# A closer scheduler model and a higher rank for readings of banks, in a hybrid MLA + DeltaNet block on one Trainium2 core

## The chip, the cores and the metric

The kernel runs on one core of a Trainium2 chip. A core has five engines with instruction streams of their own: TensorE (PE: matmuls, with the weight loads PEld beside them), VectorE (DVE), ScalarE (ACT), GpSimd (POOL) and SyncE (SP), which issues transfers. The metric is the device time of one execution in microseconds (us).

## The reference

One layer of a decoder block with 512 tokens, width 2048 and float32 throughout:

```python
def block(x, c, p):                         # x (512, 2048)
    sh_a, sc_a, gt_a, sh_f, sc_f, gt_f = split(silu(c) @ w_mod + b_mod)
    h = rmsnorm(x) * (1 + sc_a) + sh_a
    cq, ckv, kpe, q, k, v, z, b, a, ga, gb = split(h @ w_in)
    ya = mla(cq, ckv, kpe) @ ...            # 8 heads, causal softmax, low-rank q and kv, rotary part
    yb = gdn(conv_silu(q, k, v), z, b, a)   # gated DeltaNet, 8 heads, chunks of 64
    x  = x + gt_a * ((sigmoid(ga) * ya + sigmoid(gb) * yb) @ w_o)
    h2 = rmsnorm(x) * (1 + sc_f) + sh_f
    g, u = split(h2 @ w_gate_up)            # 2 x 5632
    return x + gt_f * ((silu(g) * u) @ w_down)
```

## The kernel before, in words

TensorE multiplies float32 values as pairs: each operand is split into a rounded part `hi` and a rest `lo`, and a product is three matmuls (hi x hi, hi x lo, lo x hi). A weight tile is loaded from memory into a buffer `raw` (5 of them); ScalarE makes `hi` by a cast (`halves`, L263) and VectorE makes `lo = raw - hi` (L264); there are 4 buffers each for `hi` and `lo`. The 16 row blocks of the width are called k. The gate and up projections (`big(s)`, s = 1 to 10), w_o and w_down use Strassen's seven products on halves, which need sums of weight tiles (L1826, L2014) ahead of the split (L1847/1848, L2022/2023).

The work is written as Units (load, split, matmuls, then `post`) which a `Driver` emits in turn: weights are loaded and split a few units ahead, and side chains (statistics, the DeltaNet's solve, attention, normalization) are stepped on after every 12 matmuls. Matmul results lie in 8 PSUM banks, which VectorE or ScalarE has to read ("evict") before the bank is used again. Side results that TensorE itself reads stand on the same two engines.

The order on each engine is set in two ways. TensorE, GpSimd and SyncE are pinned: their instructions keep the order of the program text. VectorE and ScalarE are not: when the kernel is built, the Tile scheduler lists their instructions by priority on a model of the machine, and then the order is fixed. An engine runs its instructions strictly in that order, and waits at the first one whose inputs aren't there.

The steps that the change and the prediction touch:
- start: the parts of w_mod are multiplied by a broadcast `cbc` (L435) and summed (`mod_sum`, L449); `scaled_h` makes h from x and scale (`hh` on ScalarE, L506, `hl` on VectorE, L508); the first weight is split in two parts (L307).
- normalized tokens: when the row norm `r_all` is there, `full_h` (L513, 515, 516) makes the full h for all 16 k.
- low-rank norm: squares of cq and ckv (L991), the copies out of the banks (L992), a scale `rs` by Newton steps (L417, `rsqrt` L229 to 233), its use (L1001); then TensorE transposes ckv (`cT`).
- DeltaNet: the solve of small triangles (`fsX`, `fsT`, L820/822), `T` assembled by copies (L868/869) from its results, which return by DMA; sums `acc` of the convolution (L396, 398).
- attention: softmax (L1187 to 1193), transposes (L1204), values.
- w_o: `add_gated` (L1432) adds the bank to x, squares (L1442/1444) follow, and TensorE sums them (`hss`), from which `part_rstd` makes the row norm of the second half; h2 is normalized (`h2_gen`).
- big(s): the evictions `after` (L1865 to 1879); in `strassen`, `after` (L2038).
- end: `token_unit` squares x (L2377) and scales xo (L2350).

Of the kernel before, what the change touches and what calls it, by code (L numbers as in the profile page):

```python
# [11 lines left out]
AF = mybir.ActivationFunctionType  # L12
ALU = mybir.AluOpType
# [16 lines left out]
AHEAD = 2  # L30
LOADS = 4
GROUP = 12


class Unit:
# [136 lines left out]
def block_kernel(ctx: ExitStack, tc: tile.TileContext, a: dict, out, out_t):  # L172
    nc = Core(tc, PINNED)
# [16 lines left out]
    def S(s, dt=F32):  # L190
        return slots.tile([P, 512], dt, tag="s", name=nm(s))
# [15 lines left out]
    def tok(j):  # L207
        return slice(j * P, (j + 1) * P)

    def h4(ap):  # L210
        return ap.rearrange("p (h d) -> p h d", h=4)

# [67 lines left out]
    def fm_set(name, loads, width, kt, x, done, ks=None, lo_eng=None, st=None, small=False, cols=slice(0, T), alone=False, late=False,  # L280
               in_parts=()):
        widths = [min(P, width - o) for o in range(0, width, P)]
        st = {} if st is None else st

        def unit(k0, nk):
            box = {}

            def start():
                box["raw"] = fetch(loads(k0, nk), width, nk, small)

            def split():
                box["w"] = halves(box.pop("raw"), width, nk, nc.gpsimd if lo_eng and k0 % 4 == 0 else None, small)

            if in_parts and k0 == 0:
                def start():
                    raw = box["raw"] = raws.tile([P, nk, width], F32, tag="raw", name=nm("raw"))
                    for dst, src in loads(k0, nk):
                        for cs in in_parts:
                            load(dst(raw)[:, :, cs], src[:, :, cs])

                def split(between):
                    raw = box.pop("raw")
                    hi = his.tile([P, nk, width], F32R, tag="hi", name=nm("hi"))
                    lo = los.tile([P, nk, width], F32R, tag="lo", name=nm("lo"))
                    box["w"] = hi, lo
                    for i, cs in enumerate(in_parts):
                        nc.scalar.copy(hi[:, :, cs], raw[:, :, cs])  # L307
                        if i == 0:
                            between[0]()
                        nc.vector.tensor_tensor(lo[:, :, cs], raw[:, :, cs], hi[:, :, cs].bitcast(F32), ALU.subtract)  # L310
                        if i == 0:
                            between[1]()

            def pre():
                if k0 == 0 and cols.start == 0:
                    st["ps"] = [PS(name) for _ in widths]

            mms = []
            for kk in range(nk):
                k = k0 + kk  # L320
                for j, wd in enumerate(widths):
                    sl = slice(j * P, j * P + wd)
                    mms += three(
                        lambda j=j, wd=wd: st["ps"][j][:wd, cols],
                        lambda kk=kk, sl=sl: box["w"][0][:, kk, sl], lambda kk=kk, sl=sl: box["w"][1][:, kk, sl],
                        lambda k=k: x(k)[0], lambda k=k: x(k)[1],
                        k == 0, k == kt - 1)

            def post():
                if k0 + nk == kt and done is not None:  # L330
                    done(st["ps"])
                    drv.hold()

            return Unit(start, split, mms, pre, post, alone=alone, late=late and k0 + nk == kt)

        return [unit(k0, nk) for k0, nk in ks or [(k, 2) for k in range(0, kt, 2)]]

    def tm_set(name, loads, kt, x, done, nk=2, ts=tuple(range(NT)), lo_eng=None, weight=1, alone=False, xt=None):
        st = {}
        if xt is None:  # L340
            def xt(k, t):
                return [v[:, tok(t)] for v in x(k)]

        def unit(k0):
            box = {}

            def start():
                box["raw"] = fetch(loads(k0, nk), 512, nk)

            def split():  # L350
                box["w"] = halves(box.pop("raw"), 512, nk, nc.gpsimd if lo_eng and k0 % 4 == 0 else None)

            def pre():
                if k0 == 0:
                    st["ps"] = {t: PS(name) for t in ts}

            mms = []
            for kk in range(nk):
                k = k0 + kk
                for t in ts:  # L360
                    mms += three(
                        lambda t=t: st["ps"][t][:],
                        lambda k=k, t=t: xt(k, t)[0], lambda k=k, t=t: xt(k, t)[1],
                        lambda kk=kk: box["w"][0][:, kk, :], lambda kk=kk: box["w"][1][:, kk, :],
                        k == 0, k == kt - 1)

            def post():
                if k0 + nk == kt:
                    done(st["ps"])
                    drv.hold()  # L370

            return Unit(start, split, mms, pre, post, weight=weight, alone=alone)

        return [unit(k0) for k0 in range(0, kt, nk)]
# [787 lines left out]
    def attention():  # L1162
# [5 lines left out]
        def scores(i):  # L1168
# [8 lines left out]
            if qb == 3:  # L1177
                del QN[h], KN[h], qpT[h]
                if h == 7:
                    kpT.clear()  # L1180

        def softmax(i):
            h, qb = items[i]
            N = (qb + 1) * P
            ps = box[i].pop("ps")
            m, s, r = (sm[:, i, j:j + 1] for j in range(3))
            nc.vector.tensor_tensor(ps[:, tok(qb)], ps[:, tok(qb)], neg, ALU.add)  # L1187
            nc.vector.tensor_reduce(m, ps[:, 0:N], AX.X, ALU.max)
            nc.vector.tensor_scalar(m, m, -scale, None, op0=ALU.mult)
            p = S("P")  # L1190
            nc.scalar.activation(p[:, 0:N], ps[:, 0:N], AF.Exp, bias=m, scale=scale, accum_out=s)
            nc.vector.reciprocal(r, s)
            nc.vector.tensor_scalar(p[:, 0:N], p[:, 0:N], r, None, op0=ALU.mult)
            box[i]["p"] = p

        def transposes(i):
            h, qb = items[i]
            N = (qb + 1) * P
            p = box[i].pop("p")
            ps = PS("pT")  # L1200
            for kb in range(qb + 1):
                nc.tensor.transpose(ps[:, tok(kb)], p[:, tok(kb)], ident)
            s = S("pT")
            (nc.scalar.copy if i % 2 else nc.vector.tensor_copy)(s[:, 0:N], ps[:, 0:N])  # L1204
            box[i]["pT"] = s

        def values(i):
            h, qb = items[i]
            s = box[i].pop("pT")
            if qb == 0:  # L1210
                yps[h] = PS("yT")
            for kb in range(qb + 1):
                mm(yps[h][:, tok(qb)], V[h // 4][kb][:, tok(h % 4)], s[:, tok(kb)], start=kb == 0, stop=kb == qb)
            if qb == 3:
                yT[h] = hilo(yps.pop(h)[:], "y")
                if h % 4 == 3:
                    del V[h // 4]
# [189 lines left out]
    x2 = [[None] * 8 for _ in range(2)]  # L1407
    s_ffn, sh_ffn, gt_mix, gt_ffn, gt_neg, gt_mneg = (C(n, [P, 16]) for n in ("s_ffn", "sh_ffn", "gt_mix", "gt_ffn", "gt_neg", "gt_mneg"))
# [29 lines left out]
    def squares(q, seg, eng):  # L1438
# [6 lines left out]
        else:  # L1445
            st.append(s)

    def part_rstd(segs):

        ps = PS("hss")  # L1450
# [37 lines left out]
    def half_sets(name, loads, x, done):  # L1488
# [3 lines left out]
        def unit(h, k0):  # L1492
# [20 lines left out]

            def post():
                if k0 + 2 == KT:
                    done(h, st[h])
                    st[h] = None
                    drv.hold()

# [208 lines left out]
    def half_of(tile_, k):  # L1728
        return tile_[:, 256 * (k % 2):256 * (k % 2) + 256]
# [10 lines left out]
    def start_h2(h):  # L1740
        return lambda: h2c.append(drv.add(h2_gen(h)))

    def h2_gen(h):

        yield 3 if h else 1
        diag = part_rstd([HALF[h]])
        yield 6 if h else 4
        r = spread(*diag)
        for q in range(8):
            f = S("h2f")  # L1750
            for k in (2 * q, 2 * q + 1):
                nc.vector.scalar_tensor_tensor(half_of(f, k), half_of(x2[h][q], k), s_ffn[:, k:k + 1], r, op0=ALU.mult, op1=ALU.mult)
                nc.scalar.activation(half_of(f, k), half_of(f, k), AF.Identity, bias=sh_ffn[:, k:k + 1])
            x2[h][q] = None
            h2f[h][q] = f
            h2T[h][q] = hilo(f[:], "h2")
            h2n[h] = 2 * q + 2
            yield 2

    w_gu, w_dn = a["w_gate_up"][0], a["w_down"][0]  # L1760
# [38 lines left out]
    def big(s):  # L1799
# [64 lines left out]
        def tt(o, x, y):  # L1864
            nc.vector.tensor_tensor(o, x, y[:], ALU.add)  # L1865

        def after(c, t):
            if c == "m1":
                nc.scalar.copy(v[t], ps["m1"][t][:])
# [126 lines left out]
    def strassen(w, c1, c0, products, ready, outputs, freed):  # L1996
# [6 lines left out]
        def unit(k):  # L2003
# [28 lines left out]

            res = {}

            def after(c):
                def tt(name, x, y, op):
                    s_ = res[name] = euvw[0][:, "euvw".index(name), :] if name in "euvw" else S(name)[:]
# [491 lines left out]
```

## Time and profile before

| quantity | before |
|---|---|
| runs, us | 2731.93, 2739.36, 2734.11 (median 2734.11) |
| span of the profiled execution, us | 2731.7 |
| TensorE busy, us | 2705.7 (99%) |
| VectorE busy, us | 2098.3 (77%) |
| ScalarE busy, us | 1204.9 (44%) |
| GpSimd busy, us | 258.8 (9%) |
| memory read and written, MB | 476.62 and 83.89 |

The page gives the span of one profiled execution, which is 2.4 us under the median of the runs. Busy is the time in which an engine had an instruction under way; matmuls overlap at their ends, so that a busy TensorE is not one at its peak rate. Start times in the rows count from the start of the span. In a row, "out<-in" are the names of the tiles, and the bracket at its end is the idle time of the engine before it and what ended that.

### The profile page before, as it was taken

Reading aid. Unit: us, or ns where it says so; the run is one execution under the profiler, and the core shown is the slowest. Engines: PE = TensorE matmul, PEld = TensorE weight load, DVE = VectorE, ACT = ScalarE, POOL = GpSimd, SP = SyncE. Lnnn points to the kernel's source line nnn. Section 1 sums busy time; section 2 is a strip of 40 time slices with the busy share of each in tenths; the row PEclk is TensorE's granted clock in tenths of the full one; section 3 lists DMA queues with packets and bytes.
Section 4 is the critical chain, followed back from the end, with each engine's and each line's share of the span. In section 5 each row is a group of like instructions: output and inputs, shape, how many; then the busy total and the mean of one; then the engine's idle time right before and its main releaser. Section 6 shows DMA issues by size and latency. Waiting matters only on the chain.

```text
span 2731.7 us, 41089 instructions
## 1 busy us (share of the span) xinstructions
PE 2705.7 (99%) x15304; PEld 2351.8 (86%) x15304; DVE 2098.3 (77%) x3361; ACT 1204.9 (44%) x1717; POOL 258.8 (9%) x361
## 2 busy tenths in 40 slices
PE   9999999999999999999999999999999999999998
PEld 7888788888888888889999888888888888998997
DVE  8784656677977886788787877778787777877877
ACT  3443432442344343234473444444444446446445
POOL 0000011102101000001000000000000103113113
PEclk9999999999999999999999999999999999999999
DMA  9896455646666978725854556665655668569565
GB/s 364 302 357 215 143 177 173 190 144 185 198 187 194 315 253 313 258 78 131 268 185 136 195 201 208 204 208 198 212 190 198 214 212 208 132 194 202 126 190 178
DMA packets 315489, 562.20 MB, mean 206 GB/s; under 512 B 40772, under 2 KB 120916, under 8 KB 315288
## 3 DMA queue, kind: packets, MB, share of 16 engines
q1 hardware_dynamic: 264776, 458.99, 51.6%
q0 software_dynamic: 31872, 74.76, 10.6%
q10 hardware_dynamic: 18640, 25.83, 2.7%
q8 instruction: 120, 1.97, 0.3%
q14 instruction: 81, 0.66, 0.1%
HBM read 476.62 MB, written 83.89 MB: 205 GB/s over the span
## 4 chain that ended last, share of the span: by engine, by line
PE 90%; DVE 4%; DMA 3%; issue 2%; ACT 1%; SPq 0%; DVEq 0%; ACTq 0%; POOL 0%
PE m L155 41%; PE gb L155 6%; PE v L155 4%; PE gu L155 3%; PE z L155 3%; PE ya L155 3%; PE k L155 3%; PE q L155 3%; PE yb L155 3%; PE dn L155 3%; PE s L155 3%; PE ckv L155 2%; PE cq L155 2%; PE wo L155 1%; PE qk L155 1%
## 5 line engine op out<-in xcount | busy, mean ns | idle before, releaser
L263 ACT CAST hi<-raw 128x1024 fp32r<-128x1024 f32 x249 | 258.8, 1041 | 538.9 <-DMA raw<-in_w_in_dram 164.9
L264 DVE TENSOR_TENSOR lo<-raw,hi 128x1024 fp32r<-128x1024 f32 x249 | 302.6, 1216 | 202.4 <-ACT hi L263 197.6
L1847 ACT CAST hi<-raws 128x512 fp32r<-128x512 f32 (+1 forms) x240 | 218.6, 911 | 328.0 <-PE m L155 269.2
L1848 DVE TENSOR_TENSOR lo<-raws,hi 128x512 fp32r<-128x512 f32 (+1 forms) x240 | 247.4, 1042 | 83.9 <-ACT hi L1847 83.6
L155 PE MATMUL m<-xh,lo 128*128 128x256 f32 x1088 | 308.4, 283 | 1.3 <-DVE lo L2023 1.3
L155 PE MATMUL m<-xh,hi 128*128 128x256 f32 x1088 | 308.1, 283 | 1.5 <-ACT hi L2022 1.5
L155 PE MATMUL m<-xl,hi 128*128 128x256 f32 x1088 | 307.9, 283 | 0.0
L449 DVE CUSTOM_DVE_ANT_0 rawm<-rawm,cbc 128x1024 f32<-128x1024 f32 x192 | 232.1, 1230 | 2.0 <-DMA rawm<-in_w_mod_dram 1.7
L155 PEld LDWEIGHTS m<-xh,lo 128*128 128x128 f32 x1088 | 208.8, 192 | 2.0 <-DVE lo L2023 1.9
L155 PEld LDWEIGHTS m<-xh,hi 128*128 128x128 f32 x1088 | 208.9, 192 | 1.7 <-ACT hi L2022 1.7
L155 PEld LDWEIGHTS m<-xl,hi 128*128 128x128 f32 x1088 | 208.9, 192 | 0.1
L155 PE MATMUL m<-hi,h2h 128*128 128x512 f32 x480 | 190.1, 396 | 0.0
L155 PE MATMUL m<-hi,h2l 128*128 128x512 f32 x480 | 187.2, 390 | 0.0
L155 PE MATMUL m<-lo,h2h 128*128 128x512 f32 x480 | 187.2, 390 | 0.0
L2022 ACT CAST hi<-sums 128x1024 fp32r<-128x1024 f32 x88 | 92.2, 1048 | 134.4 <-PE m L155 102.4
L2023 DVE TENSOR_TENSOR lo<-sums,hi 128x1024 fp32r<-128x1024 f32 x88 | 107.4, 1220 | 45.5 <-ACT hi L2022 45.4
L1847 ACT CAST hi<-sums 128x1024 fp32r<-128x1024 f32 x80 | 84.2, 1053 | 109.4 <-PE m L155 104.5
L1848 DVE TENSOR_TENSOR lo<-sums,hi 128x1024 fp32r<-128x1024 f32 x80 | 97.6, 1220 | 26.7 <-ACT hi L1847 26.1
L155 PEld LDWEIGHTS m<-hi,h2l 128*128 128x128 f32 x480 | 90.1, 188 | 19.0
L155 PEld LDWEIGHTS m<-hi,h2h 128*128 128x128 f32 x480 | 90.2, 188 | 18.5 <-DVE euvw L1865 0.7
L155 PEld LDWEIGHTS m<-lo,h2h 128*128 128x128 f32 x480 | 90.3, 188 | 17.5
L2022 ACT CAST hi<-raws 128x768 fp32r<-128x768 f32 x88 | 73.4, 835 | 66.8 <-PE m L155 48.1
(581 smaller groups left out, 7418.3 us busy)
## 6 DMA issues: line engine op xcount, KB each, us to landing
raws<-in_w_gate_up_dram SPq DMA_DIRECT2D x400, 256.0 KB, 3.6
rawm<-in_w_mod_dram SPq DMA_DIRECT2D x192, 512.0 KB, 5.4
raw<-in_w_in_dram SPq DMA_DIRECT2D x143, 512.0 KB, 4.6
raws<-in_w_down_dram SPq DMA_DIRECT2D x128, 256.0 KB, 3.9
s_dram<-raws POOLq DMA_DIRECT2D x80, 256.0 KB, 2.3
raws<-s_dram SPq DMA_DIRECT2D x80, 256.0 KB, 3.3
rawa<-in_w_in_dram SPq DMA_DIRECT2D x32, 512.0 KB, 4.6
raws<-in_w_o_dram SPq DMA_DIRECT2D x48, 256.0 KB, 3.1
```

Source lines behind the costliest of these rows:

```text
L155: return self.tc.keep_in_program_order(f(*args, **kwargs))
L263: nc.scalar.copy(hi[:], raw[:])
L264: (lo_eng or nc.vector).tensor_tensor(lo[:], raw[:], hi[:].bitcast(F32), ALU.subtract)
L449: r = nc.vector.tensor_tensor_reduce(raw, raw, c, 1.0, 0.0, ALU.mult, ALU.add, parts[:, k, half:half + 1])
L1847: nc.scalar.copy(hi[:], src)
L1848: nc.vector.tensor_tensor(lo[:], src, hi[:].bitcast(F32), ALU.subtract)
L2022: nc.scalar.copy(hi[:], src)
L2023: nc.vector.tensor_tensor(lo[:], src, hi[:].bitcast(F32), ALU.subtract)
```

## The change

The list of edits: (1) the scheduler is told to use a closer model of the machine's time (`schedule_with_timeline_sim=True`); (2) a wrapper `soon` lifts the priority of what it wraps by 600 (`SOON`): the readings of banks (`done` of the sets, `after` in big and strassen), softmax, transposes and values of attention, the row norm's `part_rstd`, and the normalization of the tokens h2, whose body becomes a function `normalize`. The pinned engines keep their order, and no operation is added or removed: between the two built programs 736 VectorE and 196 ScalarE instructions stand at another place.

```diff
+SOON = 600
...
+    def soon(f):
+
+        def g(*args, **kwargs):
+            with tc.high_priority(SOON):
+                return f(*args, **kwargs)
+        return g
...
             def post():                      # fm_set; tm_set alike
                 if k0 + nk == kt and done is not None:
-                    done(st["ps"])
+                    soon(done)(st["ps"])
                     drv.hold()
...
+        @soon
         def softmax(i):
...
+        @soon
         def transposes(i):
...
+        @soon
         def values(i):
...
+    @soon
     def part_rstd(segs):
...
             def post():                      # half_sets
                 if k0 + 2 == KT:
-                    done(h, st[h])
+                    soon(done)(h, st[h])
...
+    @soon
+    def normalize(h, q, r):
+        f = S("h2f")
+        for k in (2 * q, 2 * q + 1):
+            nc.vector.scalar_tensor_tensor(half_of(f, k), half_of(x2[h][q], k), s_ffn[:, k:k + 1], r, op0=ALU.mult, op1=ALU.mult)
+            nc.scalar.activation(half_of(f, k), half_of(f, k), AF.Identity, bias=sh_ffn[:, k:k + 1])
+        x2[h][q] = None
+        h2f[h][q] = f
+        h2T[h][q] = hilo(f[:], "h2")
+        h2n[h] = 2 * q + 2
...
         for q in range(8):
-            f = S("h2f")
...
+            normalize(h, q, r)
             yield 2
...
+        @soon
         def after(c, t):                     # big
...
+            @soon
             def after(c):                    # strassen
...
-    with tile.TileContext(nc) as tc:
+    with tile.TileContext(nc, schedule_with_timeline_sim=True) as tc:
```

More of the change, by code (lines that the diff above doesn't have):

```diff
@@ L368, in post @@
                 if k0 + nk == kt:
-                    done(st["ps"])
+                    soon(done)(st["ps"])
                     drv.hold()
@@ L1749, in h2_gen @@
         for q in range(8):
-            f = S("h2f")
[L1751 to L1757, printed above, removed]
+            normalize(h, q, r)
             yield 2
```

## The prediction

> **What bounds the kernel now.** I read the header and the busy totals of the page first, then the chain of work that ended last, then the waits of TensorE, then a table of windows over the places where the order moves.
>
> ```profile
> span 2731.7 us, 41089 instructions
> PE 2705.7 (99%) x15304; PEld 2351.8 (86%) x15304; DVE 2098.3 (77%) x3361; ACT 1204.9 (44%) x1717; POOL 258.8 (9%) x361
> PE 90%; DVE 4%; DMA 3%; issue 2%; ACT 1%; SPq 0%; DVEq 0%; ACTq 0%; POOL 0%
> ```
>
> TensorE (PE) is busy for 2705.7 of 2731.7 us, so at most 26 us could ever be won by reordering the other engines, and some of that is the start and the end, where no matmul can run. VectorE (DVE) is at 77%, not a bound on average. The waits of TensorE for other engines, as (total, times, longest), show how little is left:
>
> ```profile
> PE hss L155 <- DVE sq L1444: 2.2, 1, 2.2
> PE dn L155 <- DVE g L2038: 1.7, 1, 1.7
> ...
> PE cq L155 <- ACT sz L962: 0.9, 1, 0.9
> ```
>
> These are single waits. An order that served TensorE perfectly would win a few such waits. An order that serves it badly in one place can lose more there than all of them together, because a matmul that comes late is never made up by an engine that is 99% full. The windows show where VectorE has no room (columns: window, length, then busy and count of PE, PEld, DVE, ACT, POOL, then granted clock, DMA share, GB/s):
>
> ```profile
> 160.00:206.00 46.00, 45.04 (x199) 36.93 (x198) 44.13 (x65) 22.18 (x29) 2.13 (x4) 1.00 0.99 367
> 690.00:750.00 60.00, 60.00 (x325) 49.56 (x323) 57.76 (x154) 20.20 (x37) 6.79 (x10) 1.00 0.69 210
> ...
> 1358.00:1362.00 4.00, 4.00 (x21) 4.00 (x22) 2.52 (x5) 0.09 (x1) 0.00 (x0) 0.58 0.68 221
> 1400.00:2255.00 855.00, 854.97 (x4128) 720.03 (x4127) 669.59 (x786) 391.90 (x482) 65.97 (x121) 1.00 0.60 198
> ```
>
> At 160 to 206 and at 690 to 750 VectorE is busy for 96% of the time. There, whatever is put in front of a step delays that step by its full length. In the big loop (1400 to 2255) it has 22% free.
>
> **The change, part by part.** No operation is added or removed. Laid side by side, the two built programs have the same instructions on each engine; TensorE, SyncE and GpSimd keep their order to the instruction, 736 VectorE and 196 ScalarE instructions stand elsewhere. So every cost is a delay: the length of what now stands in front of a step, less the slack that step had. I went through the places where the new order puts other work ahead of something that TensorE reads.
>
> *The start.* ScalarE now has the split of the first weight (hi L307, which waits for its DMA) ahead of the third and fourth part of cbc, and VectorE has the two sums L449 of the next k ahead of the first hl.
>
> ```profile
> 8.46 0.41 ACT L307 CAST hi<-raw 128x256 fp32r<-128x256 f32 x1 [1.25 <-DMA raw<-in_w_in_dram]
> ...
> 7.55 1.23 DVE L449 CUSTOM_DVE_ANT_0 rawm<-rawm,cbc 128x1024 f32<-128x1024 f32 x1
> 11.19 0.74 DVE L508 SCALAR_TENSOR_TENSOR hl<-xT,s_mix,hh 128x512 fp32r<-128x512 f32 x1
> ...
> 11.99 0.50 PE L155 MATMUL s<-hl,hi 128*128 128x512 f32 x1 [0.53 <-DVE hl L508]
> ```
>
> The second half of the first L449 waits for cbc until about 10.75 instead of 7.55 (3.2 later), two L449 at 1.15 come in between: hl ends some 4.9 later, TensorE goes on at 16.9 instead of 11.99. This is not a term of its own, because the next place is paced by VectorE and the DMAs and swallows it.
>
> *Normalized tokens at 160 to 190 us.* When r_all arrives, full_h runs for 16 k: L513 scales x (16 times) and L516 makes hl. Before, only four of each were done when the third lo of the next weights (L264) was made.
>
> ```profile
> 162.49 2.07 DVE L513 SCALAR_TENSOR_TENSOR xT<-xT,s_mix,r_all 128x512 f32<-128x512 f32 x3
> 164.48 1.22 DVE L264 TENSOR_TENSOR lo<-raw,hi 128x1024 fp32r<-128x1024 f32 x1
> 165.62 0.74 DVE L516 SCALAR_TENSOR_TENSOR hl<-xT,sh_mix,hh 128x512 fp32r<-128x512 f32 x1
> ...
> 177.26 1.23 DVE L264 TENSOR_TENSOR lo<-raw,hi 128x1024 fp32r<-128x1024 f32 x1 [1.87 <-ACT hi L263]
> ...
> 178.71 0.39 PE L155 MATMUL ga<-hh,lo 128*128 128x512 f32 x1
> ...
> 185.28 0.51 PE L155 MATMUL ga<-hh,lo 128*128 128x512 f32 x1 [0.96 <-DVE lo L264]
> ```
>
> Now all 16 L513 and 12 L516 stand ahead of that lo: 12 + 8 = 20 more. Three L513 take 164.48 - 162.49 = 1.99, so 0.663 each: 13.3 us. VectorE idled 1.87 before the lo at 177.26, which is filled: 11.4 later. TensorE read that lo 0.2 after its end: 11.2 late. The idle 0.96 at 185.28 closes, since the later tiles are then ready: +10.2, the start's 4.9 within it.
>
> *ckv and the solve, 734 to 765 us.* ScalarE now has the cast hi L263, which waits for a buffer that TensorE frees, ahead of the four L991 (squares of ckv); the scale rs of L417 follows, and L1001 applies it.
>
> ```profile
> 735.15 0.59 ACT L991 ACTIVATE junk<-ckv 128x512 f32<-128x512 f32 x1
> 740.83 1.06 ACT L263 CAST hi<-raw 128x1024 fp32r<-128x1024 f32 x1 [2.33 <-PE z L155]
> ...
> 735.86 2.60 DVE L992 COPY ckv<-ckv 128x512 f32<-128x512 f32 x4 [1.06 <-ACT junk L991]
> 738.38 0.16 DVE L417 TENSOR_SCALAR rs<-st_c 128x4 f32<-128x4 f32 x1
> 740.12 0.74 DVE L398 SCALAR_TENSOR_TENSOR acc<-rawa,sh_mix,acc 128x512 f32<-128x512 f32 x1
> 740.86 1.08 DVE L868 COPY T<-T 32x256 f32<-32x256 f32 x1
> 746.98 1.64 DVE L1001 TENSOR_SCALAR ckv<-ckv,rs 128x512 f32<-128x512 f32 x4
> ...
> 754.17 0.60 PE L155 MATMUL cT<-kc,ckv 128*128 128x128 f32 x4
> ```
>
> The copies L992 ended at 735.86 + 2.60 = 738.46 and now end about 746.6, 8.1 later: four squares behind a cast that itself ends near 741.9. The chain from rs to L1001 then shares VectorE with twelve L398 and L396 (0.68 each, 7.9), two lo L264 (1.15 each, 2.3), eight copies of T (2.5 with the long first), T32T, M and kpl (1.9), and its own small steps (about 0.7 beyond overlap): 15.3, and L1001 takes 1.64. It ends at 746.6 + 15.3 + 1.64 = 763.5. TensorE wanted it at 754.17 less its pass of 0.2: +9.1. Beside it, the solve (L820/822) gives way to lo L264 and ends about 12 later than
>
> ```profile
> 728.81 0.18 DVE L822 TENSOR_TENSOR fsX<-fsX,fsT 128x16 f32<-128x16 f32 x1
> ```
>
> so T, which returns by DMA and is first used at 740.86, comes later too, and with it what TensorE makes of T: 1.5 to 2.6 before cT. I take the lower end, since part of it lies beside the wait for L1001: **+10.6** for this place.
>
> *The clock after a stall.* The window 1358 to 1362 above follows a wait of 2.25 us of TensorE and has a granted clock of 0.58: 4 us x 0.42 = 1.7 us of matmul time lost. Two new stalls of some 10 us cost that each: +3.4. [...]
>
> *Evictions of w_o at 1349 to 1388.* Four add_gated (L1432), with their bank just finished, now stand ahead of a lo L264, and a lo stands among the squares of the row sum hss.
>
> ```profile
> 1347.93 1.23 DVE L264 TENSOR_TENSOR lo<-raw,hi 128x1024 fp32r<-128x1024 f32 x1 [0.79 <-ACT hi L263]
> ...
> 1358.00 1.27 PE L155 MATMUL hss<-ones,sq 128*128 128x1 f32 x8 [2.25 <-DVE sq L1444]
> ...
> 1385.28 0.68 DVE L1444 TENSOR_TENSOR sq<-sq,sq 128x512 f32<-128x512 f32 x1
> ...
> 1386.92 0.95 PE L155 MATMUL hss<-ones,sq 128*128 128x1 f32 x8
> ```
>
> The delayed lo stalls TensorE about 2 us, which comes out of the 2.25 that it waited at hss anyway; the squares end one lo later, 1.1. The second hss had 1386.92 - 1385.96 = 0.96 of slack and its last square now stands behind two lo and the work on h2, 3.2 later: 2.3. Together **+3.4**.
>
> *The big loop, ten rounds.* The evictions were to gain rank, yet a lo now stands ahead of the second of four L1865.
>
> ```profile
> 1517.18 2.47 DVE L1865 TENSOR_TENSOR euvw<-euvw,m 128x512 f32<-128x512 f32 x4
> ...
> 1518.79 0.40 PE L155 MATMUL m<-hi,h2h 128*128 128x512 f32 x1
> ...
> 1550.20 1.22 DVE L1826 TENSOR_TENSOR sums<-raws,raws 128x1024 f32<-128x1024 f32 x1
> ```
>
> The first L1865 ends near 1517.85 and the second near 1518.46, 0.33 before TensorE reuses the bank at 1518.79; 0.6 more in front leaves 0.3 late. In the second place of a round the pair stands behind the sums at 1550.20 (1.22) and a lo, 3.1 to 4.9 later against a slack of 3.8: 0 to 1.1. I take 0.35 a round: **+3.5**, with the bounds 0 and 15.
>
> *The rest.* Read in the same way, without rows here, w_down (2310 to 2343) has splits xl and sums of the next weights ahead of its lo L2023, which end 1.8 later than TensorE's use allows: +1.8, between 0 and 4. Attention has delays of up to 0.7 in several places, 3.7 in all, less 1.8 of waits that vanish: +1.9, between -1.8 and 3.7. The wait for sz (0.9 above) and two smaller ones beside it go: -1.6. At the end:
>
> ```profile
> 2721.47 1.32 ACT L2350 ACTIVATE xo<-xo,rs 128x512 f32<-128x512 f32 x2
> 2722.69 0.40 ACT L2377 ACTIVATE dn<-x2t 128x256 f32<-128x256 f32 x1
> ```
>
> Four xo (0.66 each, 2.6) stand ahead of the last square L2377 where two did: 1 to 2.5, I take **+2.0**.
>
> The sum: 10.2 + 10.6 + 3.4 + 3.4 + 3.5 + 1.8 + 1.9 - 1.6 + 2.0 = 35.2, on the span 2731.7: 2766.9. The median of the runs, 2734.11, lies 2.4 above the profiled span, so the forecast is 2769.
>
> **The rivals.** *Faster.* The new order does what its rank promises: readings of banks and squares come first, the waits for hss, dn, sz and some small ones go (2.2 + 1.7 + 0.9, with the rest under 10 in all), and nothing new is late. It decides at the two crowded places: if r_all arrived 11 us sooner at 162, or the cast L263 didn't hold up the squares at 735. Neither is seen, VectorE is at 96% in both windows and the r_all chain is fed by matmuls in an unchanged order. It would give about 2725; chance 0.06.
>
> *Nothing.* The orders differ only among steps with slack: 2734 within 8 us (0.3% is about what a measurement can tell from no change). The two delays of 10 us would both have to be hidden; chance 0.05.
>
> *Half.* The moved steps were late for the order because of waits of their own, so the two crowded places cost about half (5 each, a stall short enough for less clock loss) and the small ones hide: +10 + 1.7 + 5 = 16, 2750; chance 0.22.
>
> *Dearer.* In the big loop VectorE waits for weights,
>
> ```profile
> DVE raws L1826 <- DMA raws<-in_w_gate_up_dram: 60.1, 49, 2.2
> ```
>
> 1.2 us each time, up to 2.2. Where an eviction stands behind such a sum it inherits that wait: 1.2 more in each of ten rounds, with a clock drop of 1.7 in some of them, 20 in all: 2790; chance 0.15.
>
> **How the numbers follow.** The forecast, 2769, has the remaining 0.52; its own range, with the bounds of the big loop, of w_down and of the solve, is 2757 to 2782. Low is 2744, inside "half"; high is 2800, above "dearer" with one more clock loss a round. That leaves out the cases faster and nothing (0.11) and the ends of the others. Faster by more than 0.3% 0.06, within it 0.06 (nothing, and the lowest of half), slower 0.88.
>
> **What would show it.** Right: waits of TensorE for lo L264 of 5 to 11 us near 170 to 190, and for ckv L1001 near 754 of about 9; a granted clock below 1 for some 3.4 us behind each; all other engines' busy times unchanged, and TensorE's busy time as before but for the clock. The waits for sz and g L2038 smaller or gone, and that for hss near 1.1 longer in total. Wrong: no wait over 3 us in those two places, or new waits of ten equal sizes in the big loop that outweigh them.

## The result and the profile after

The changed kernel took 2794.74 us (median of 4 runs, 2793.01 to 2797.88), the kernel before 2736.28 in the runs beside it. The ratio is 1.0219 (95% interval 1.0204 to 1.0233): 59 us slower, where 35 were forecast. The profiled execution after has a span of 2791.2 us, 59.5 above that of before.

The page of the changed kernel, the lines that answer to those of before (the third gives shares of the chain of work that ended last):

```profile
span 2791.2 us, 41122 instructions
PE 2727.4 (98%) x15304; PEld 2360.4 (85%) x15304; DVE 2092.0 (75%) x3361; ACT 1202.8 (43%) x1717; POOL 257.9 (9%) x361
PE 60%; issue 25%; DVE 6%; DMA 5%; POOL 2%; ACT 1%; SPq 0%; POOLq 0%; DVEq 0%; ACTq 0%
```

VectorE and ScalarE are as busy as before, to 6.3 us. TensorE is busy 21.7 us longer with the same 15,304 matmuls. The mean granted clock fell from 0.998 to 0.991: by the trace's record of the granted clock, 34.4 us of matmul time ran at a granted clock of 0.50 where it had been 3.4. Half of the difference, taken as lost, makes 15.5 us of the 21.7. The rest was not taken apart; a first matmul behind a wait, for one, takes 0.50 us in the rows below and not 0.39. The other 38 us are time in which TensorE is not busy. Its waits in the changed kernel (total, times, longest; the wait for crow is the kernel's start and was there before; line 156 is the former 155, and later lines move by 8 to 18):

```profile
PE m L156 <- DVE euvw L1881: 16.3, 21, 2.2
PE cT L156 <- DVE ckv L1009: 7.6, 1, 7.6
PE ga L156 <- DVE lo L272: 4.6, 2, 2.8
PE s L156 <- ACT hh L514: 3.6, 1, 3.6
PE hss L156 <- DVE sq L1455: 3.3, 2, 2.1
PE cb L156 <- DMA crow<-in_c_dram: 3.0, 1, 3.0
PE s L156 <- DVE s_mix L463: 2.9, 1, 2.9
PE wo L156 <- DVE lo L272: 1.9, 1, 1.9
```

The first line is the big loop's evictions; before, no such line was there. Since both executions have the same matmul records in the same order, the start of each matmul after less its start before says how late TensorE is at that point. What each stretch added, in us:

| stretch (time of before, us) | forecast | in the changed kernel | that stretch's new order alone (runs below) |
|---|---|---|---|
| 0 to 206, start and normalized tokens | +10.2, clock +1.7 | +13.7 | +18.3 |
| 688 to 775, ckv and the solve | +10.6, clock +1.7 | +10.0 | +9.8 |
| 800 to 1000, attention | +1.9 | +1.0 | |
| 1097, sums of ya and yb | 0 | +2.7 | |
| 1340 to 1400, evictions of w_o, hss | +3.4 | +6.5 | |
| 1400 to 2262, big loop | +3.5 | +27.9 | +31.4 |
| 2262 to the last matmul | +1.8 | -4.5 | |
| cq | -1.6 | 0 | |
| behind the last matmul | +2.0 | +2.0 | |

The measured terms add up to 59.3. The last column, and the us given with ratios below, are the ratio less one, times 2734.

Three places in rows of the changed kernel. At the ckv norm, the four squares L999 stand behind a cast that waits for TensorE; the copies end at 760.17, and the scale that then starts is used 15.1 us later:

```profile
754.65 1.05 ACT L271 CAST hi<-raw 128x1024 fp32r<-128x1024 f32 x1 [4.38 <-PE z L156]
755.60 0.59 ACT L999 ACTIVATE junk<-ckv 128x512 f32<-128x512 f32 x1
...
759.48 0.69 DVE L1000 COPY ckv<-ckv 128x512 f32<-128x512 f32 x1
760.08 0.30 DVE L425 TENSOR_SCALAR rs<-st_c 128x4 f32<-128x4 f32 x1
775.20 1.67 DVE L1009 TENSOR_SCALAR ckv<-ckv,rs 128x512 f32<-128x512 f32 x4
...
775.73 1.66 PE L156 MATMUL cT<-kc,ckv 128*128 128x128 f32 x4 [7.59 <-DVE ckv L1009]
```

Ahead of the four evictions L1881 in the second round of the big loop, VectorE in the changed kernel:

```profile
1619.41 0.69 DVE L1842 TENSOR_TENSOR raws<-raws,raws 128x512 f32<-128x512 f32 x1 [2.56 <-DMA raws<-in_w_gate_up_dram]
1620.02 1.22 DVE L1864 TENSOR_TENSOR lo<-raws,hi 128x1024 fp32r<-128x1024 f32 x1
...
1629.33 0.69 DVE L1842 TENSOR_TENSOR raws<-raws,raws 128x512 f32<-128x512 f32 x1 [2.66 <-DMA raws<-in_w_gate_up_dram]
1629.94 1.22 DVE L1864 TENSOR_TENSOR lo<-raws,hi 128x1024 fp32r<-128x1024 f32 x1
1631.08 1.28 DVE L1888 TENSOR_TENSOR euvw<-euvw,m 128x512 f32<-128x512 f32 x2
1632.27 0.68 DVE L1881 TENSOR_TENSOR euvw<-euvw,m 128x512 f32<-128x512 f32 x1
1632.87 0.68 DVE L1864 TENSOR_TENSOR lo<-raws,hi 128x512 fp32r<-128x512 f32 x1
...
1633.01 0.66 PE L156 MATMUL m<-hi,h2h 128*128 128x512 f32 x1 [2.20 <-DVE euvw L1881]
```

The same stretch before:

```profile
1580.64 1.23 DVE L1848 TENSOR_TENSOR lo<-raws,hi 128x1024 fp32r<-128x1024 f32 x1 [0.27 <-ACT hi L1847]
1582.13 0.69 DVE L1826 TENSOR_TENSOR raws<-raws,raws 128x512 f32<-128x512 f32 x1 [0.27 <-DMA raws<-in_w_gate_up_dram]
...
1587.67 0.69 DVE L1826 TENSOR_TENSOR raws<-raws,raws 128x512 f32<-128x512 f32 x1 [1.08 <-DMA raws<-in_w_gate_up_dram]
1590.17 0.69 DVE L1826 TENSOR_TENSOR raws<-raws,raws 128x512 f32<-128x512 f32 x1 [1.81 <-DMA raws<-in_w_gate_up_dram]
```

The lo at 1580.64 and the sum at 1582.13 have changed places. The sum waits for its weights, the lo waits behind it, and it ends 3.0 us later against TensorE. That lo is the last reader of a buffer raws, so SyncE issues the next load later too, in the changed kernel right behind it:

```profile
1621.27 0.33 SPq L156 DMA_DIRECT2D raws<-s_dram  x1
```

The loads then come later, the sum at 1629.33 waits for one of them, and the evictions behind that sum find TensorE waiting. The low clock behind such stalls, in windows of the changed kernel (columns as in the prediction):

```profile
774.00:781.00 7.00, 5.27 (x16) 3.83 (x17) 5.60 (x11) 0.69 (x1) 0.00 (x0) 0.58 1.15 276
1417.00:1424.00 7.00, 6.20 (x30) 6.24 (x31) 5.02 (x16) 2.82 (x5) 0.00 (x0) 0.58 0.28 88
1632.00:1637.00 5.00, 3.99 (x10) 2.94 (x11) 4.69 (x8) 0.00 (x0) 0.00 (x0) 0.66 0.47 157
```

Not every wait is followed by it. Two waits of much the same length, in two rounds of the loop:

```profile
2117.86 0.50 PE L156 MATMUL m<-hi,h2h 128*128 128x512 f32 x1 [1.46 <-DVE euvw L1881]
...
2198.12 0.50 PE L156 MATMUL m<-hi,h2h 128*128 128x512 f32 x1 [1.40 <-DVE euvw L1881]
```

The clock stayed up behind the first and fell behind the second:

```profile
2114.47:2117.88 3.41, 1.96 (x10) 1.30 (x8) 3.41 (x6) 1.67 (x2) 0.00 (x0) 1.00 0.23 60
2117.88:2121.29 3.41, 3.18 (x13) 2.33 (x14) 3.24 (x6) 0.00 (x0) 0.00 (x0) 1.00 0.47 171
2196.39:2199.80 3.41, 1.77 (x7) 0.93 (x6) 3.41 (x7) 0.68 (x2) 0.00 (x0) 1.00 0.70 220
2199.80:2203.21 3.41, 3.41 (x10) 2.66 (x9) 2.92 (x5) 0.04 (x1) 0.00 (x0) 0.50 0.03 11
```

The last window is the stretch of low clock in the trace's record, and the others have its length and lie whole multiples of it ahead. While matmuls run, the record of the changed kernel shows eight stretches at 0.50. Four last 6.83 us, from 15.27, 189.35, 773.03 and 1418.15, and four last 3.41, from 1387.43, 1633.19, 2035.96 and 2199.80. The record of before has one, of 3.41 us from 1358.62. In the changed kernel the distances between those starts are 51, 171, 180, 9, 63, 118 and 48 times 3.413 us, in order of time. The length of a wait alone doesn't tell whether the clock falls: the window ahead of the drop held 1.64 us of idle time (the wait of 1.40 and a second one of 0.24), the one that held the wait of 1.46 held 1.45. What does tell was not shown.

### The profile page after: what moved, and what is told of

Read it like the earlier page. It is cut to its first block, busy times and chain, and to the rows that moved or that the text cites. A ratio compares the mean times of both kernels' runs of the same rounds, so it can differ in the third digit from the quotient of the medians.

```text
span 2791.2 us, 41122 instructions
## 1 busy us (share of the span) xinstructions
PE 2727.4 (98%) x15304; PEld 2360.4 (85%) x15304; DVE 2092.0 (75%) x3361; ACT 1202.8 (43%) x1717; POOL 257.9 (9%) x361
## 4 chain that ended last, share of the span: by engine, by line
PE 60%; issue 25%; DVE 6%; DMA 5%; POOL 2%; ACT 1%; SPq 0%; POOLq 0%; DVEq 0%; ACTq 0%
PE m L156 18%; PE gb L156 5%; PE v L156 4%; PE s L156 3%; PE k L156 3%; PE dn L156 3%; PE q L156 3%; PE yb L156 3%; PE ya L156 3%; PE z L156 3%; DMA raws<-in_w_gate_up_dram 2%; PE ga L156 2%; PE ckv L156 2%; PE cq L156 2%; DVE lo L1864 1%
## 5 line engine op out<-in xcount | busy, mean ns | idle before, releaser
L1842 DVE TENSOR_TENSOR raws<-raws,raws 128x512 f32<-128x512 f32 x80 | 55.3, 691 | 82.2 <-DMA raws<-in_w_gate_up_dram 81.6
L1842 DVE TENSOR_TENSOR sums<-raws,raws 128x1024 f32<-128x1024 f32 x80 | 97.7, 1222 | 18.7 <-DMA raws<-in_w_gate_up_dram 17.6
```

Source lines behind the costliest of these rows:

```text
L1842: add = lambda o, x, y: nc.vector.tensor_tensor(o, x, y, ALU.add)
```

## The experiments

**Model or rank.** Two kernels have one half of the change each.

```diff
 model_only, against the kernel before
-    with tile.TileContext(nc) as tc:
+    with tile.TileContext(nc, schedule_with_timeline_sim=True) as tc:
 rank_only, against the changed kernel
-    with tile.TileContext(nc, schedule_with_timeline_sim=True) as tc:
+    with tile.TileContext(nc) as tc:
```

> The kernel before with the closer scheduler model alone, no raised rank. Theory (the model makes the new order, the rank next to nothing: with the model on, a handful of instructions stand elsewhere with and without the rank): the changed kernel's time, 2794 within 8 us, with TensorE waiting for ckv L1001 near 754 and for the evictions of the big loop as there. Rival (the rank pushes evictions and normalized tokens into the way): most of the loss is gone, under 2755.

2794.19 us, ratio 1.0213 (1.0198 to 1.0228).

> The raised rank alone, on the scheduler's old model. Theory (the model makes the loss): about 150 instructions move, none in the big loop between 1400 and 2255 us and none before 650 us that TensorE needs, so 2735 within 8 us. Rival (the rank causes the delays of the row norm and the evictions): over 2760.

2736.90 us, ratio 1.0003 (0.9993 to 1.0012). The whole loss is the scheduler's closer model. The raised rank costs nothing that can be measured, with the old model, and changes next to nothing under the new one. The waits of the kernel with the model alone read like those of the changed kernel:

```profile
PE m L155 <- DVE euvw L1865: 18.3, 19, 2.5
PE cT L155 <- DVE ckv L1001: 7.7, 1, 7.7
PE ga L155 <- DVE lo L264: 5.4, 2, 3.9
```

**The places one by one.** All other kernels are the kernel before, with the order of VectorE and ScalarE written out: each instruction is tied behind the one that is to precede it, by an edge that sets the order of issue and adds no wait. With that, a stretch of the new order can be put into the old one. Holding an order costs nothing that can be measured: b_loopY and b_loopW below, held in nearly the old order, have the time of the kernel before (ratios 1.0005 and 1.0006).

```diff
+        traced = [i for i in block if i.engine == engine]
...
+        for a, b in zip(order, order[1:]):
+            tc.add_manual_dep(b, a.name, mybir.DependencyInfo(mybir.DependencyClass.NoSync, mybir.DependencyReason.DATA),
+                              reason="hold_order")
 b_start:  the new order from 0 to 206 us
 b_norm:   the new order from 150 to 206 us
 b_ckv:    the new order from 688 to 775 us
 b_loop:   the new order from 1400 to 2262 us
 b_gain:   the new order from 60 to 145, 880 to 915 and 2430 to 2700 us
```

> The kernel before in its old order, but in the changed kernel's order from 0 to 206 us (start and normalized tokens). Theory (the delays of the start and of 160 to 190 us are the order's own): TensorE 13.7 us late at 206 and never earlier again, 2748 within 4 us. Rival (VectorE and the transfers catch up, since the old order behind it has slack): under 2742.

2752.24 us, ratio 1.0067 (1.0052 to 1.0082): 18 us, just above the range expected. In the profiled execution TensorE is 20.0 us late at 206, not 13.7.

> The kernel before in its old order, but in the changed kernel's order from 150 to 206 us (normalized tokens), with the old start. Prediction's step (20 scalings and hl more ahead of the third lo, 11.2 us late, of which 10.2 stay; the start's delay lies within it): 2744 to 2748. Rival (the start's 7.6 us and this place's delays add, as with both in the new order it was 18 slower): 2741 to 2746, with a TensorE delay at 206 us of 6 to 10 us, some 8 below that of both.

2752.84 us, ratio 1.0065 (1.0050 to 1.0080). That is above both ranges, with TensorE 18.6 us late at 206. The place alone costs as much as with the new start ahead of it, so in these two kernels the start's delay, 7.6 us by the trace of b_start, lies within the delay behind it, as the prediction had it. For the changed kernel no run shows that by itself, since both held kernels are 4 to 6 us above its 13.7. In b_norm ScalarE stands at two issues of spills, of hl and then of hh:

```profile
172.66 0.72 ACT L515 ACTIVATE hh<-xT,sh_mix 128x512 fp32r<-128x512 f32 x1 [0.46 <-DVE xT L513]
180.32 0.33 ACTq L1598 DMA_DIRECT2D hspill<-hl  x1
183.36 0.33 ACTq L1598 DMA_DIRECT2D hspill<-hh  x1
183.73 0.73 ACT L515 ACTIVATE hh<-xT,sh_mix 128x512 fp32r<-128x512 f32 x1 [10.35 <-DMA hspill<-hl]
```

No hh could be made for 10.35 us; in b_start the same wait took 10.29, and the changed kernel has none like it there. The built programs show a reason: these issues also wait for an earlier transfer, and which one is given out when the kernel is built. The spill of hl waits for a spill of hh in the changed kernel and for a load of weights in b_norm and b_start. So a held order isn't a full copy of the changed kernel here. That this wait is the whole difference was not tried.

> The kernel before in its old order, but in the changed kernel's order from 688 to 775 us (the low-rank norm of ckv and the DeltaNet's solve). Theory: TensorE waits 7 to 9 us for ckv L1001 near 754, and 1.7 to 2.2 go by at the low clock: 2744 within 3 us. Rival (in the changed kernel the place was worse for the delays ahead of it): under 2740.

2743.06 us, ratio 1.0036 (1.0023 to 1.0049): 9.8 us, with one wait of 7.6 us for ckv, as in the changed kernel.

> The kernel before, VectorE and ScalarE held in a written order: the old one, but the changed kernel's between 1400 and 2262 us (the ten rounds of the big loop). Theory (the order inside the loop costs what TensorE lost there in the profile, 27.6 us from 34.4 to 62.0 late): 2762 within 5 us. Rival (part of that loss is later transfers after the earlier delays, or chance in the landing of the weights, and not the loop's order): 2736 to 2750.

2766.53 us, ratio 1.0115 (1.0100 to 1.0131). The loop's own order makes the loop's loss, 31.4 us here; it needs no delay ahead of it.

**Inside the loop.** Four kernels with single moves of VectorE's order.

```diff
 b_loopX, eight rounds
-lo L1848, sum L1826 (waits for its weights)
+sum L1826 (waits for its weights), lo L1848
 b_loopY, ten rounds
-L1865, L1865, L1865, L1865, lo L1848
+L1865, lo L1848, L1865, L1865, L1865
 b_loopW, each round's start, products L1896 of the round before
-lo, L1896, sum, lo, sum, lo, L1896, sum, lo, sum, lo, L1896, sum, lo, sum, lo, L1896
+lo, L1896, sum, L1896, L1896, lo, L1896, sum, lo, sum, lo, sum, lo, sum, lo, sum, lo
 b_loopXYW: all three
```

> The kernel before in its old order, with one swap made in each of eight rounds of the big loop: a weight sum L1826 that waits for its transfer is put ahead of the lo L1848 that it followed before. Theory (the late lo frees its buffer late, the next weights are loaded late, the sums ahead of the evictions wait for them and so do the evictions): TensorE loses 1 to 2 us in each of the eight rounds at the evictions L1865, 8 to 16 us in all, 2743 to 2751. Rival (the lo between the evictions makes the loss, this swap has slack): 2734 to 2738.

2741.63 us, ratio 1.0025 (1.0015 to 1.0034): 6.8 us. One swap of two neighbours, eight times. The second round in b_loopX:

```profile
1583.89 0.69 DVE L1826 TENSOR_TENSOR raws<-raws,raws 128x512 f32<-128x512 f32 x1 [1.99 <-DMA raws<-in_w_gate_up_dram]
1584.50 1.22 DVE L1848 TENSOR_TENSOR lo<-raws,hi 128x1024 fp32r<-128x1024 f32 x1
...
1592.06 0.69 DVE L1826 TENSOR_TENSOR raws<-raws,raws 128x512 f32<-128x512 f32 x1 [3.75 <-DMA raws<-in_w_gate_up_dram]
1593.93 0.69 DVE L1826 TENSOR_TENSOR raws<-raws,raws 128x512 f32<-128x512 f32 x1 [1.18 <-DMA raws<-in_w_gate_up_dram]
...
1597.60 0.50 PE L155 MATMUL m<-hi,h2h 128*128 128x512 f32 x1 [1.49 <-DVE euvw L1865]
```

The chain is there by itself: lo late, load late, sum late (3.75 idle, where there were 1.08 at that sum before), evictions late, TensorE waits. The size is under the range expected, 8 to 16 us, and above the rival's: the profiled execution has 5 waits at the evictions, 4.0 us in all, and not one in each of the eight rounds. No transfer of this built program waits for another earlier one than before, so the swap alone does it.

> The kernel before in its old order, with one move in each of the ten rounds of the big loop: the first lo L1848 behind the four evictions L1865 is put between the first and the second of them. Theory of the prediction (0.6 us more ahead of the second eviction against 0.33 of slack): 0.3 to 0.4 a round, 3 to 4 us in all, 2737 to 2740. Rival (this lo alone makes the stalls of 1.1 to 2.4 us that the changed kernel shows there): 2748 to 2762.

2736.07 us, ratio 1.0005 (0.9996 to 1.0014). No loss that can be told from none, and not over 3.8 us. The prediction's 3.5 us for this step is neither shown nor excluded, and the step is not what makes the loop's loss.

> The kernel before in its old order, with one move in the big loop: the products L1896 of the round before (and their Silu) ahead of the sums and lo that they followed. Theory (every lo of the first half of a round is then 0.6 to 2 us late, which is within the slack of the evictions so long as nothing else is late): 2735 to 2742. Rival (this move alone makes the stalls): 2755 to 2766.

2736.09 us, ratio 1.0006 (0.9997 to 1.0015). Within the slack, as expected.

> The kernel before in its old order, with three moves in the big loop: a sum that waits for its transfer ahead of a lo (8 rounds), a lo between the evictions L1865 (10 rounds), and the four products L1896 of the round before ahead of the sums and lo that they followed, with their Silu on ScalarE (each round). Theory (together these delay lo, loads, sums and so the evictions as the changed kernel's loop does, 31.5 us slower): at least two thirds of it, 2755 to 2768. Rival (each adds alone, 6.6 for the first and 1.9 for the second, and the third has slack): 2741 to 2746. Another (the rest of the loop's new order, sums ahead of lo behind the evictions, makes the loss): 2743 to 2752.

2746.56 us, ratio 1.0043 (1.0029 to 1.0057): 11.8 us, a little over a third of the loop's 31.4. The theory asked for two thirds and fell; the three moves do little more than add (6.8, 1.4 and 1.6 alone). What the rest is can be seen in part: against TensorE, the first L1865 of rounds 2 to 9 starts on average 1.05 us later than before in b_loopX, 1.13 in b_loopXYW and 2.2 in b_loop. The moves that are left (sums ahead of lo behind the evictions and at a round's start, swaps in the first and last round) go with the other 1 us. Which of them makes it stays open; 23 of the loop's 639 transfers also wait for another earlier one in b_loop.

**The gains.** In three places TensorE was less late behind the new order than ahead of it.

> The kernel before in its old order, but in the changed kernel's order in the places where TensorE was less late behind them than ahead: 60 to 145, 880 to 915 and 2430 to 2700 us. Theory (these gains are the order's own: 1.2, 1.8 and 4.0 us): 7 us faster, 2727 to 2732. Rival (TensorE won there only because it came later, so that what it waited for was there): 2733 to 2738.

2729.20 us, ratio 0.9981 (0.9971 to 0.9991): 5 us of the 7 expected are won by the order itself. The last kernel adds one more edit by hand:

```diff
 b_best, on top of b_gain, VectorE at 1350 us
-L1432, L1444, L1444, L1444, L1432, lo L264, L1444
+L1432, L1432, L1444, L1444, L1444, L1444, lo L264
```

> The order that was 5 us faster (the old one, the changed kernel's in 60 to 145, 880 to 915 and 2430 to 2700 us), and at 1350 us the four evictions L1432 and six squares L1444 without the lo L264 between them, which TensorE reads only at 1362. Theory (the wait for hss, 2.25 us, is the squares' place on VectorE): the wait falls by about 1.1 us and the low clock behind it may go (1.7): 2725 to 2729. Rival (the last eviction or its square waits for something else): 2729 to 2731.

2725.58 us, ratio 0.9962 (0.9949 to 0.9976), faster than both kernels, by 10 us against before and 69 against the changed one. How much of that is the last edit is less sure, since the intervals of b_gain and b_best overlap. The wait for hss is 1.24 us (2.25 in the kernel before, 2.4 in b_gain), but the low clock behind it stayed, 0.60 in the window from 1355 to 1359:

```profile
1355.12 1.23 PE L155 MATMUL hss<-ones,sq 128*128 128x1 f32 x8 [1.24 <-DVE sq L1444]
```

## Why the prediction was right, and where it was off

The direction was right, and so was the mechanism: a step of TensorE's queued behind work that now stands ahead of it. The two places that were put first cost about what was said. The time lies inside the whole range, 2744 to 2800, but 26 us above the forecast and above the 2757 to 2782 of the forecast's own case, and nearly all of that is one term. It stayed inside only because the range reached past the rival "dearer". Two of the signs named in advance came out against the forecast: no wait for lo of 5 to 11 us near 170 to 190 (the longest is 2.79), and in the big loop new waits of 16.3 us, though not of equal sizes, that outweigh those of the two places (13.3).

*ckv and the solve* came out as worked: copies 7.9 us later against TensorE (8.1 forecast: they end 21.7 us later, of which TensorE's own lateness ahead of this place is 13.8), 15.1 us from the scale to its use (15.3 forecast). The wait was 7.6 instead of 9.1: the sum counted all four L1009 (L1001 before), and cT begins at 775.73 while they run until 776.87. The 1.5 for what TensorE makes of T came to nothing; there is no wait for it. The clock cost about 2.1 (4.1 us of matmul time at 0.50) instead of 1.7.

*Start and normalized tokens* together cost 13.7 against 11.9. The composition was not as forecast: in the changed kernel 6.2 of the start's 7.5 us were still there at 160 us, and TensorE's waits behind that were 1.76 (lo), 1.15 (hi) and 2.79 us (lo) rather than one of 11; the low clock took 2.4 us more. That the sum came so near is in part luck.

*The big loop* is the step that failed: 27.9 us where 3.5 was taken and 15 was the upper bound. The prediction priced the order by the slack of the second eviction (0.33 us) and by a lo of 0.6 us. The first one has less slack. Before, it ends at 1517.18 + 0.68 = 1517.86, and TensorE reuses its bank at

```profile
1518.09 0.39 PE L155 MATMUL m<-hi,h2h 128*128 128x512 f32 x1
```

which leaves 0.23 us in this round; over the ten rounds it is 0.06 to 1.21. Ahead of the evictions stands, in both orders, a sum that waits for its weights. What delays a load there by more than this slack reaches TensorE, and so a swap 12 us earlier, between instructions that TensorE doesn't read at that time, can cost it. The swaps explain 6.8 us of the loop's loss, the three moves together 11.8 of 31.4; which moves make the rest stays open. Of the 27.9, 16.3 are the waits at the evictions and 5.1 the low clock behind three of them. The rival "dearer" named that wait and the clock drops (20 us, 2790), and had 0.15; but it had the evictions newly put behind such a sum, and they stood there before as well. What spoke for it in the rows was the idle time of 60.1 us at those sums: the forecast took the free time of VectorE in the loop as room, and where it is a wait for weights it is the sign that the evictions hang on the transfers.

*The clock* was taken as 3.4 us for two stalls. It was 15.5, for 34.4 us of matmul time at 0.50 and not 3.4: the low stretches at 15, 189, 773 and 1418 us last 6.83 us each, and the sum had taken its 1.7 a stall from one that lasts 3.41, at 1358.62 before. The clock had been seen low there behind a wait of 2.25 us, and yet the places with stalls of 2 us were priced without it. The length of a wait was no sure guide to it either: one of 1.40 us at 2198 was followed by the low clock and one of 1.46 us at 2117 was not.

*Evictions of w_o* cost 6.5: the stalls were as forecast (1.93 for the lo, against which the hss wait fell from 2.25 to 1.23, and 2.1 at the second hss), and the rest is the clock behind the second hss, 0.58 in the window at 1417. *The end* cost the 2.0 that were forecast. *w_down* won 4.5 us where 1.8 were to be lost, since the waits for g (from 1.7 to 0.3) and at 2655 (1.5) shrank or went. In b_gain, too, TensorE gains 1.9 us at 2655; for g it isn't shown, since b_gain's wait is 1.0 and kernels with the old order there have 0.7 to 1.7. The wait for sz stayed, so its 1.6 was no gain. The 2.7 at 1097, where ol and sig stand later, was missed.

"Nothing", "half" and "faster" are out by the result. That the raised rank does nothing was no rival and should have been: the two halves of the change were never costed apart.

## What to carry to other kernels

When an order is worked out by a model, price a moved step by what hangs on it as well as by its length: a lo that frees a buffer moves a load, and a load moves whatever stands behind the instruction that waits for it (6.8 us in b_loopX, for one swap in each of eight rounds). The evictions here stand behind a sum that waits for its weights, and had 0.06 to 1.21 us of slack. A change with two halves should be built both ways before it is priced, and where a new order is better in some places only, it can be held there by order edges and left out elsewhere, which gave 10 us here.

## What was not expected of the hardware

In the changed kernel the granted clock fell to 0.50 for 3.41 us behind a wait of 1.40 us, and stayed at 1.00 behind one of 1.46. In b_best it was 0.60 from 1355 to 1359, behind a wait of 1.24 us for hss and with eight matmuls of one column in 1.23 us. What decides whether it falls was not measured.

In b_norm an issue held up ScalarE though its data were ready: the hl to be spilled was written by 174.06, its spill went out at 180.32, and ScalarE made nothing for 10.35 us. By the built program it also waits for a load of weights. Of the 1,754 transfers of this kernel, 326 wait for another earlier one after the change, although those of SyncE and GpSimd keep their order and only 29 of ScalarE's 133 stand at another place.
